# Moving the result's store, the semaphore clear and the last wait of a log-sum-exp kernel to SyncE

## Chip, cores, metric

One core of a Trainium2 chip. The metric is the device time of one execution in microseconds, the median of several. Each execution also has a span: the time from the start of the kernel's first instruction to the end of its last one. Time minus span is therefore what lies outside the kernel's own instructions. All runs quoted were with a granted clock of 1.0.

## The reference

```python
batch, seq, dim = 32, 512, 1024          # x: float32
x_max = np.max(x, axis=axis, keepdims=True)
return (x_max.squeeze(axis) + np.log(np.sum(np.exp(x - x_max), axis=axis))).astype(np.float32)
```

So 67.11 MB are read and 64 KB written. The kernel leaves out the maximum (the inputs are normal draws) and computes log(sum(exp(x))).

## The kernel before

Each of 128 partitions holds 128 rows of 1024 values. SyncE loads them in 17 chunks into a ring of 51 rows; ScalarE takes the exponential, VectorE (for some rows ScalarE's own accumulator) sums, and ScalarE takes the logarithm in three pieces. The last piece covers the last 4 rows and ends all arithmetic. Then comes the part in question:

```python
    take_logs(late_row, NB, late[:, : NB - late_row], dves, acts)   # last logarithm, on ScalarE
    nc.scalar.wait_ge(act_done, acts)
    nc.scalar.dma_start(out=out_v, in_=res).then_inc(stored, 16)    # 128 rows of 512 B
    nc.scalar.sem_clear(range(used[0], used[-1] + 1))               # 19 semaphores to zero
    # ... (cut) the first load is moved ahead of the opening barrier ...
    tc.close()                     # emits two exit barriers over all five engines
    tc.compile()
    nc.gpsimd.wait_ge(stored, 16)  # behind the barriers: is the store in memory?
    nc.gpsimd.sem_inc(stored, -16)
```

In the program this gives: store, clear, two exit barriers (each engine reports to GpSimd, GpSimd releases all), and one last instruction on GpSimd that waits for the store. Hiding the barriers behind the flight of the store is already part of the kernel before.

The softmax here doesn't subtract the row's maximum and nothing guards it: scores larger than these inputs give would overflow.

## Time and profile before

| what | value |
|---|---|
| median time | 163.15 us (3 runs, 163.01 to 163.37) |
| span of the profiled run (its time 163.28) | 161.41 us |
| end of the last logarithm | 159.76 us |
| last of 16 landings of the store | 161.37 us |
| end of GpSimd's wait, which is the end of the span | 161.41 us |

The rows of a source line in the profile give the engine, the operation, a count, durations in ns (minimum/median/maximum) and the first and last start in us. A "q" after an engine's name marks its instruction queue (waits, barriers, DMA issues), which is not counted as busy. The barriers consist of DRAIN and EVENT_SEMAPHORE instructions, with which the engines report, wait and are released. "Landing" is the time from the issue of a transfer to the last report that its data have arrived. The lines that carry the argument stand in the prediction. Behind the end of the span the trace holds one more thing, the times of semaphore updates; the prediction reads them too.

### The profile page before, as it was taken

The numbers are of one execution on the slowest core, as the hardware profiler recorded it, in microseconds if no ns is written. First come the engines' busy times: TensorE is split into PE (matmuls) and PEld (weight loads), VectorE is DVE, ScalarE is ACT, GpSimd is POOL, SyncE is SP. The second block draws the span as 40 slices with busy tenths as digits, with TensorE's granted clock in tenths as the row PEclk, the third lists the DMA queues.
The fourth block names the chain that finished last, engine by engine and source line by source line (L and its number), as shares of the span: only waits on it lengthen the run. The fifth ranks groups of instructions, "written<-read, shape, count | busy, mean of one in ns | idle before, by whom it ended". The sixth has DMA issues, their size and how long they took to land.

```text
span 161.4 us, 149 instructions
## 1 busy us (share of the span) xinstructions
DVE 121.0 (75%) x46; ACT 115.1 (71%) x40; POOL 0.2 (0%) x4
## 2 busy tenths in 40 slices
DVE  0028000003999999999999699999999999999892
ACT  3170005996079960999519993999199999999995
POOL 0000000000000000000000000000000000000000
DMA  6999699989989989989979999999999999999990
GB/s 256 508 487 457 289 472 520 406 374 520 422 357 520 406 374 520 406 374 520 406 341 455 455 455 439 422 422 422 430 429 429 418 426 415 427 430 417 403 394 24
DMA packets 2592, 67.18 MB, mean 416 GB/s; under 512 B 288, under 2 KB 416, under 8 KB 928
## 3 DMA queue, kind: packets, MB, share of 16 engines
q1 hardware_dynamic: 2448, 67.11, 96.9%
q10 hardware_dynamic: 144, 0.07, 0.1%
HBM read 67.11 MB, written 0.07 MB: 416 GB/s over the span
## 4 chain that ended last, share of the span: by engine, by line
DMA 49%; DVE 29%; ACT 20%; issue 0%
DMA ring<-in_x_dram 49%; DVE sums L154 29%; ACT ring L134 17%; ACT ring L161 3%; ACT res L105 0%
## 5 line engine op out<-in xcount | busy, mean ns | idle before, releaser
L154 DVE TENSOR_REDUCE sums<-ring 128x8 f32<-128x8192 f32 (+5 forms) x14 | 111.2, 7995 | 37.3 <-ACT ring L134 37.2
L134 ACT ACTIVATE ring<-ring 128x8192 f32<-128x8192 f32 (+6 forms) x18 | 104.4, 5835 | 43.9 <-DMA ring<-in_x_dram 43.8
L141 DVE CUSTOM_DVE_ANT_0 ring<-ring 128x512 f32<-128x512 f32 x16 | 9.9, 688 | 0.0
L161 ACT ACTIVATE ring<-ring 128x1024 f32<-128x1024 f32 x9 | 9.3, 1041 | 0.0
L119 ACT ACT_TABLE_LOAD x1 | 1.3, 1283 | 0.8 <-PEq L215 0.8
L161 ACT ACTIVATION_READ_ACCUMULATOR ring<-ring 128x1 f32 x9 | 1.5, 172 | 0.0
L141 DVE DVE_READ_ACCUMULATOR2_ANT sums<- 128x1 f32 x16 | 1.3, 84 | 0.0
L105 ACT ACTIVATE res<-sums 128x81 f32<-128x81 f32 (+1 forms) x2 | 0.5, 246 | 0.0
L105 ACT ACTIVATE res<-late 128x4 f32<-128x4 f32 x1 | 0.2, 173 | 0.0
L215 POOL MEMSET const-bfloat16-1.0<- 128x1 bf16 x1 | 0.1, 103 | 0.0
L215 POOL MEMSET const-uint8-127<- 128x1 uint8 x1 | 0.1, 102 | 0.0
L215 POOL MEMSET const-float32-0.0<- 128x1 f32 x1 | 0.1, 100 | 0.2 <-issue 0.2
L215 POOL MEMSET const-float32-1.0<- 128x1 f32 x1 | 0.1, 99 | 0.0
## 6 DMA issues: line engine op xcount, KB each, us to landing
ring<-in_x_dram SPq DMA_DIRECT2D x1, 7680.0 KB, 25.2
ring<-in_x_dram SPq DMA_DIRECT2D x1, 7168.0 KB, 28.6
ring<-in_x_dram SPq DMA_DIRECT2D x1, 6656.0 KB, 35.7
ring<-in_x_dram SPq DMA_DIRECT2D x1, 4608.0 KB, 20.2
ring<-in_x_dram SPq DMA_DIRECT2D x2, 2048.0 KB, 16.1
ring<-in_x_dram SPq DMA_DIRECT2D x1, 3584.0 KB, 28.3
ring<-in_x_dram SPq DMA_DIRECT2D x1, 2560.0 KB, 27.3
ring<-in_x_dram SPq DMA_DIRECT2D x4, 512.0 KB, 27.0
```

The lines of the kernel that those rows point to most:

```text
L105: nc.scalar.activation(out=res[:, lo:hi], in_=src, func=Ln).then_inc(act_done, 1)
L119: nc.scalar.preload_act_table_set("natural_log_exp_and_others")
L134: nc.scalar.activation(out=ring[:, s + lo : s + hi], in_=ring[:, s + lo : s + hi], func=Exp).then_inc(act_done, 1)
L141: nc.vector.tensor_tensor_reduce(out=ring[:, s + j, : D // 2], in0=ring[:, s + j, : D // 2], in1=ring[:, s + j, D // 2 :], scale=1.0, scal ...
L154: nc.vector.reduce_sum(out=sums[:, row + lo : row + hi], in_=ring[:, s + lo : s + hi], axis=AX).then_inc(dve_done, 1)
L161: nc.scalar.activation(out=ring[:, s + j], in_=ring[:, s + j], func=Exp, accum_out=total(row + j),).then_inc(act_done, 1)
L215: nc = _bacc.Bacc("TRN2", target_bir_lowering=False, num_devices=1)
```

## The change

Its intent: let the engine that has been idle since the last load issue the store, clear the semaphores, and also stand in the last wait, in place of ScalarE and GpSimd. Nothing else is touched.

```diff
-    nc.scalar.wait_ge(act_done, acts)
-    nc.scalar.dma_start(out=out_v, in_=res).then_inc(stored, 16)
-    nc.scalar.sem_clear(range(used[0], used[-1] + 1))
+    nc.sync.wait_ge(act_done, acts)
+    nc.sync.dma_start(out=out_v, in_=res).then_inc(stored, 16)
+    nc.sync.sem_clear(range(used[0], used[-1] + 1))
 ... (cut)
-    nc.gpsimd.wait_ge(stored, 16)
-    nc.gpsimd.sem_inc(stored, -16)
+    nc.sync.wait_ge(stored, 16)
+    nc.sync.sem_inc(stored, -16)
```

## The prediction

> **What bounds the kernel now.** I read the page first, then the chain that ended last in order of time, then line by line what happens after the last arithmetic, because the change touches nothing ahead of it.
>
> ```profile
> span 161.4 us, 149 instructions
> ...
> DVE 121.0 (75%) x46; ACT 115.1 (71%) x40; POOL 0.2 (0%) x4
> ...
> DMA packets 2592, 67.18 MB, mean 416 GB/s; under 512 B 288, under 2 KB 416, under 8 KB 928
> ...
> DMA 49%; DVE 29%; ACT 20%; issue 0%
> ```
>
> Loading 67.11 MB at 416 GB/s fills 161.3 us by division: the body is bound by the input transfer, with VectorE and ScalarE close behind. The load queue's packets take 96.9% of 16 engines' span. None of this is touched. The end of the chain in order of time:
>
> ```profile
> 158.46 1.11 ACT ring L161 x2
> 159.57 0.02 issue
> 159.59 0.17 ACT res L105
> ```
>
> The arithmetic ends at 159.76 us, yet the span is 161.4. The missing 1.64 us is the store and the wait for it. Four lines show it, each from the view of one source line:
>
> ```profile
> L173 ACTq DMA_DIRECT2D out_dram<-res x1: 373/373/373, 159.8 to 159.8; - x1
> ...
> DMA to landing us min/median/max: 1.6/1.6/1.6
> ```
> ```profile
> L176 ACTq EVENT_SEMAPHORE_RANGE_CLEAR  x1: 119/119/119, 160.2 to 160.2; - x1
> ```
> ```profile
> L196 POOLq EVENT_SEMAPHORE  x4: 17/17/17, 160.4 to 160.8; - x4
> L196 SPq DRAIN  x3: 7/7/123, 130.7 to 160.6; - x3
> ...
> L196 SPq EVENT_SEMAPHORE  x2: 17/17/17, 160.5 to 160.8; - x2
> L196 ACTq EVENT_SEMAPHORE  x2: 17/17/17, 160.5 to 160.8; - x2
> ```
> ```profile
> L198 POOLq EVENT_SEMAPHORE  x1: 17/17/17, 161.4 to 161.4; - x1
> ```
>
> The reader is to see an order: the store's issue on ScalarE at 159.8, the clear at 160.2, two exit barriers finished by about 160.9, and GpSimd standing alone until its wait for the store passes at 161.4. That wait, not the barriers, closes the span. SyncE has only waited since its last load:
>
> ```profile
> L97 SPq DMA_DIRECT2D ring<-in_x_dram x17: 327/365/779, 0.0 to 130.2; - x17
> ...
> SPq L196 <- PEq L196: 29.9, 2, 29.6
> ```
>
> **Beyond the span.** The trace also keeps the times of semaphore updates after the span. On one low semaphore, which no instruction of the kernel touches, two groups of nine stand there, in us from the span's start: 161.138, 161.172, 161.970, 162.014, 162.037, 162.136, 162.174, 162.210, 162.257; and 163.046, 163.080, 163.119, 163.163, 163.186, 163.284, 163.322, 163.356, 163.403. Between them all other semaphores are cleared in five blocks. The last update, 163.40, is close to the measured 163.28 us of the profiled run, so I take this closing part to be in the metric.
>
> **What the Trainium skill says.** "Runtime: NRT & Kernel Launch", section "The ~15µs preamble/postamble breakdown", lists after the kernel a sync barrier (about 1.5 us), a semaphore reset and another barrier, and calls the barrier a serpentine over five engines with 44 ns per hop and 8 hops. The trace agrees: nine updates are five engines out and four back, and the ready second group takes 0.36 us with hops of 23 to 98 ns. "Perfetto Trace Analysis", section "Per-instruction lifecycle", says that the window shown for a DMA from SyncE or ScalarE holds descriptor generation, not the data movement; here 0.37 us is shown and the landing takes 1.6. "DMA: Bandwidth & Descriptors", section "Issuing engines are not separate DMA queues", says that DMAs of all issuers run on the same 16 engines, and that another issuer saves only sequencer time. No run has tested that for this store; the isolated load issues on SyncE (minimum 327 ns, against 373) bear on the sequencer part.
>
> **The change part by part.** The built order shows the move of exactly two instructions from ScalarE's end to SyncE's, the store and the clear; VectorE and GpSimd are unchanged there. The closing wait goes from GpSimd to SyncE.
>
> 1. The start of the store. It waits for the last logarithm's semaphore. On ScalarE the issue began 30 ns after the end of that activation; the pieces called "issue" where one engine hands to another are also 0.02 us. SyncE has been idle since 130.7 us and has nothing ahead of it. Difference: 0.
> 2. The issue. One of 0.33 us (the minimum on SyncE, which the loads issued alone have) for one of 0.37: minus 0.04 us if the data starts with it. The same 128 rows of 512 B; all loads ended long before, so nothing contends. I count minus 0.02, half, because the two forms are not alike.
> 3. Landing and wait. Unchanged, 1.6 us from issue: SyncE's wait should pass at about 161.37, and the span should be about 161.4.
> 4. Clear and barriers. The 0.12 us clear and the branch now lie on SyncE ahead of its barrier; the barriers shift by at most 0.2 us. They ended 0.5 us before the landing (160.9 against 161.39), so this is hidden.
> 5. The closing. Here is the gain. In the first closing group the first two updates come before GpSimd's wait ends, and the third stands still until 161.970: 0.56 us after GpSimd's last instruction ended (161.41). In the second group the same hop takes 39 ns. So I read GpSimd as the third of the five and the one all waited for; SyncE, I infer, is the fifth. GpSimd freed from its wait is done with its barrier at about 160.9 to 161.0 and reaches its update at about 161.5, still ahead of the landing plus SyncE's own way. TensorE, which ended at 160.90, made its update at 161.14, 0.24 us after. If SyncE needs like TensorE 0.24 us from its last instruction (161.39), it arrives at 161.63. Its update then stands at about 161.65, against 162.037 before: minus 0.39 us. All that follows (return, reset, second group, 1.37 us) is a chain from there and moves with it.
>
> Sum: minus 0.02 and minus 0.39, about minus 0.4 us. The term from TensorE is an estimate for an engine that I have not seen there, so I shade it to minus 0.35: 163.15 - 0.35 = 162.8 us, 0.2%.
>
> **The rivals.** *SyncE is as slow on the way out as GpSimd.* With 0.56 us its update is at about 161.95, against 162.037: minus 0.09, and about 163.05 us. For it: I see only GpSimd's and TensorE's own way. Against it: SyncE's queue entries in the barriers are short (7 ns drain against 34 to 41 on GpSimd). *GpSimd's way remains the bound*, with 0.56 us after a barrier that ends late: about 161.5 is 0.1 earlier than SyncE's estimate, so it may cost a little if the barriers slip, no more. *The store from SyncE is slower*: busy issues on SyncE took up to 779 ns; that would add up to 0.4 and give about 163.2. Against it: that was among queued loads at the start, this one is alone. *The tail of SyncE becomes the wait*: if its branch stalled for over 0.5 us, the barriers would pass the landing. Its first drain after the last load was at 130.7, immediately after the last issue, so no stall shows. *The gain is outside the metric*: then the time stays at 163.15.
>
> **Range and chances.** The three runs of before span 163.01 to 163.37. The mechanisms leave 162.7 to 163.2, and 0.15 us of scatter on the low side gives 162.55 to 163.2. Two per cent is 3.3 us, twice the whole stretch from the last arithmetic to the end of the span; nothing moved is that large. Chances: faster 0.01, same 0.98, slower 0.01.
>
> **What would show it.** Right: a span of 161.3 to 161.5 with the store now in SyncE's queue, an issue of 0.33 to 0.37, a landing of 1.6 after the issue, both barriers over before the landing, SyncE's wait the last instruction; and among the later updates, hops three and four early (about 161.5) and hop five alone late, 0.2 to 0.3 us after the wait. Wrong: a landing of over 1.8 us, a barrier that ends behind it, hop five 0.5 us or more behind the wait, or an earlier closing with an unchanged measured time. A load phase that differs in the trace would be scatter, as no instruction of it changed.

## The result, and the profile after

The changed kernel takes **162.55 us** (median of 6 runs, 162.46 to 162.77) against 163.19 us (6 runs, 162.96 to 163.37). The ratio is 0.9963 with a 95% interval of 0.995 to 0.9976. Ratios here are not quite the ratio of the medians. At the threshold of 2% that is "same"; it is a small gain all the same, of 0.60 us by the ratio (0.0037 times 163.19).

The end of the chain, in order of time (start, duration, what), for the changed kernel:

```profile
158.28 1.11 ACT ring L161 x2
159.39 0.02 issue
159.41 0.17 ACT res L105
```

The last logarithm ends at 159.59 us instead of 159.76, in a part that did not change. Hold on to that 0.18 us: it is scatter, as the section on the experiments shows. The lines of the store, the clear, the barriers and the last wait, changed kernel:

```profile
L173 SPq DMA_DIRECT2D out_dram<-res x1: 348/348/348, 159.6 to 159.6; - x1
...
DMA to landing us min/median/max: 1.6/1.6/1.6
```
```profile
L176 SPq EVENT_SEMAPHORE_RANGE_CLEAR  x1: 64/64/64, 160.0 to 160.0; - x1
```
```profile
L196 POOLq EVENT_SEMAPHORE  x4: 17/17/17, 160.2 to 160.6; - x4
L196 SPq DRAIN  x3: 7/7/27, 160.1 to 160.4; - x3
```
```profile
L198 SPq EVENT_SEMAPHORE  x1: 17/17/17, 161.2 to 161.2; - x1
```

The store goes out through SyncE, with the issue 25 ns shorter; it lands 1.6 us later, as before. The barriers finish by 160.7, before the landing. The wait at the end is now SyncE's. How long it stood there is in the view of waits of SyncE's queue (who waited for whom, total us, times, longest):

```profile
SPq L173 <- ACT res L105: 29.1, 1, 29.1
SPq L198 <- SPq L198: 0.5, 1, 0.5
```

The first line replaces the 29.6 us that SyncE spent in the exit barrier before: it now waits for the last logarithm. The second is half a microsecond alone behind the barriers, waiting for its own store.

Up to here almost nothing is gained: from the end of the last logarithm to the end of the span it is 1.647 us before and 1.611 after. The rest is behind the span. These are the updates of the closing semaphore, on which the engines report one after the other; the step from one update to the next is called a hop below. They are given in us counted from the end of each kernel's span, so negative ones happened while the last wait still stood (from the trace's semaphore records, the first group of nine and the last update of the second group):

```
update       1       2       3       4       5       6       7       8       9     last
before   -0.271  -0.237   0.561   0.605   0.628   0.727   0.765   0.801   0.848   1.994
after    -0.222  -0.187   0.018   0.061   0.133   0.183   0.221   0.257   0.303   1.451
```

Before, the third update comes 0.56 us after GpSimd's last instruction, and everything queues behind it. After, GpSimd has been free since its last barrier instruction; its update comes at 0.018, again 0.562 us after that instruction, and the fifth update, SyncE's, comes 0.133 us after SyncE's wait.

The whole difference between the two profiled runs, to the last update of the trace, is 163.403 - 162.648 = 0.755 us. It splits into 0.176 from the body (scatter), 0.036 from the last logarithm to the end of the wait, 0.495 from the wait to the fifth update (0.628 against 0.133), and 0.048 from the fifth update to the last (1.366 against 1.318).

### The profile page after: what moved, and what is told of

Its sections match the earlier page's. It is cut to its first block, busy times and chain, and to the rows that moved or that the text cites. A ratio compares the mean times of both kernels' runs of the same rounds, so it can differ in the third digit from the quotient of the medians.

```text
span 161.2 us, 149 instructions
## 1 busy us (share of the span) xinstructions
DVE 121.0 (75%) x46; ACT 115.1 (71%) x40; POOL 0.2 (0%) x4
## 4 chain that ended last, share of the span: by engine, by line
DMA 49%; DVE 29%; ACT 20%; issue 0%
DMA ring<-in_x_dram 49%; DVE sums L154 29%; ACT ring L134 17%; ACT ring L161 3%; ACT res L105 0%
```

## The experiments

The theory after the result: the gain belongs to the **last wait**, not to the store. The engines report in a fixed order at the program's end; what counts is the place of the waiting engine in this order and its own way there. The rival: the gain is that of the store's issue and of a ScalarE relieved of it. All kernels gave correct results.

**1. The wait alone.** Store and clear as before, on ScalarE.

```diff
-    nc.gpsimd.wait_ge(stored, 16)
-    nc.gpsimd.sem_inc(stored, -16)
+    nc.sync.wait_ge(stored, 16)
+    nc.sync.sem_inc(stored, -16)
```

> Only the closing wait moves to SyncE; store and clear stay on ScalarE. Theory (the way from the closing wait to the end is shorter on SyncE, 0.13 us against 0.56 plus two hops on GpSimd): about 0.50 us below the kernel before, 162.65 to 162.75; the fifth closing update 0.13 us after SyncE's wait. Rival (the gain comes from the store's issue on SyncE): within 0.1 us of the kernel before.

Measured 162.35 us against 162.90, ratio 0.9963 (0.995 to 0.9977), the ratio of the full change. The fifth update comes 0.133 us after the wait. The time is below the expected range, because the kernel before, too, was faster on this chip than expected.

**2. The store alone.** Store and clear on SyncE, the wait on GpSimd.

```diff
-    nc.sync.wait_ge(stored, 16)
-    nc.sync.sem_inc(stored, -16)
+    nc.gpsimd.wait_ge(stored, 16)
+    nc.gpsimd.sem_inc(stored, -16)
```

(This diff and those of 3 and 4 are against the changed kernel.)

> Only store and clear move to SyncE; the wait stays on GpSimd. Theory: 0.03 to 0.1 us below the kernel before (issue 0.35 for 0.37, landing as before), third closing update 0.56 us after GpSimd's wait. Rival (the store's issue is what counts): 0.5 us below the kernel before.

Measured 162.77 us, ratio 0.9986 (0.9974 to 0.9999). The trace gives 1.604 us from the last logarithm to the end of the wait (1.647 before), and again 0.561 us to the third update and 1.994 to the last. So the store's move is worth about 0.04 us, and the time's 0.23 us (0.0014 times 163) is largely scatter of the span. The rival falls.

**How the scatter is taken out.** Every run lists its span. In 11 runs of the kernel before the spans go from 160.9 to 161.4 us and the times from 162.79 to 163.30, but time minus span stays within 1.84 to 1.92. No instruction differs among those runs, so the half microsecond is run-to-run variation of the body. The spans are listed to 0.1 us, so a single difference is good to 0.05 us only; in the profiled runs, whose spans are known to the nanosecond, it is 1.871 us for the kernel before and 1.333 for the changed one. From here on I compare time minus span, and in the trace the stretch behind the last logarithm.

**3. The wait on VectorE, TensorE and ScalarE.** The changed kernel, with `nc.sync` in the two last lines replaced by `nc.vector`, `nc.tensor` or `nc.scalar`.

```diff
-    nc.sync.wait_ge(stored, 16)
-    nc.sync.sem_inc(stored, -16)
+    nc.vector.wait_ge(stored, 16)       # e3; nc.tensor in e4, nc.scalar in e5
+    nc.vector.sem_inc(stored, -16)
```

> The changed kernel with the closing wait on VectorE, by the theory the fourth of the five in the closing chain. Its own way out was not seen. If it is 0.2 us, the fourth update comes 0.2 us after the wait and the fifth 0.02 later: 0.1 us above the changed kernel and 0.5 below the one before. The marks ahead of the fourth must be early (the third at about 161.2 us). Rival (any engine but GpSimd is the same): equal to the changed kernel.

> The changed kernel with the closing wait on TensorE, by the theory the first in the closing chain. Its way out was 0.24 us and four hops (34, 39, 44, 23 ns) follow: the fifth update 0.38 us after the wait, so 0.24 us above the changed kernel and about 0.35 below the one before; all nine updates after the wait. Rival (any engine but GpSimd is the same): equal to the changed kernel.

> The changed kernel with the closing wait on ScalarE, by the theory the second in the closing chain. Three hops (39, 44, 23 ns) follow its update; its own way out was not seen, I guess 0.15 to 0.2 us. So the fifth update 0.26 to 0.3 us after the wait, and the measured time minus the span 1.46 to 1.50 us (1.33 in the changed kernel, 1.88 before); only the first update is early. Rival (place in the chain does not matter, only each engine's own way out): fifth update under 0.2 us after the wait.

Each kernel's last instruction stands on the engine asked for; here TensorE's (the queue is called PEld), ScalarE's and VectorE's, from the view of the wait's source line in each of the three runs:

```profile
L198 PEldq EVENT_SEMAPHORE  x1: 51/51/51, 160.9 to 160.9; - x1
```
```profile
L198 ACTq EVENT_SEMAPHORE  x1: 17/17/17, 161.0 to 161.0; - x1
```
```profile
L198 DVEq EVENT_SEMAPHORE  x1: 21/21/21, 160.9 to 160.9; - x1
```

The closing, counted from the end of each span (from the semaphore records; time minus span over all runs of the kernel):

| last wait on | the waiting engine's update | us after the wait | fifth update | last | time minus span |
|---|---|---|---|---|---|
| TensorE | 1st | 0.279 | 0.419 | 1.783 | 1.63 to 1.68 |
| ScalarE | 2nd | 0.140 | 0.245 | 1.611 | 1.51 to 1.53 |
| GpSimd (store alone) | 3rd | 0.561 | 0.629 | 1.994 | 1.87 to 1.92 |
| VectorE | 4th | 0.183 | 0.206 | 1.570 | 1.43 to 1.49 |
| SyncE (wait alone) | 5th | 0.133 | 0.133 | 1.443 | 1.28 to 1.38 |

In the two rows of VectorE and SyncE the first positive number is not the waiting engine's: the third update of VectorE's run at 0.008 and the fourth of SyncE's at 0.008 belong to engines that were already on their way. Which update is the waiting engine's can be told from the runs together: GpSimd's comes 0.561 or 0.562 us after its last instruction wherever the wait stands (it is that third update of VectorE's run), VectorE's ready hop behind it takes 43 or 44 ns (the fourth of SyncE's run), and TensorE's and ScalarE's runs leave none and one update ahead of the wait. This settles the order: TensorE, ScalarE, GpSimd, VectorE, SyncE. The median times were 162.68, 162.46, 162.77, 162.53 and 162.35 us (ScalarE's from another call). "Any engine but GpSimd is the same" is wrong by 0.34 us between SyncE and TensorE in the last update. For ScalarE the rival of this run, that the place does not matter, falls as well: 0.140 us of its own way, 0.105 for three hops, 0.245 in all, just under what I had guessed (0.26 to 0.3). For TensorE I had expected the fifth update at 0.38; it came at 0.419, because TensorE's update came 0.279 us after its wait, where it comes 0.235 after its last barrier instruction in the kernel before. So TensorE's figure is not the same behind every instruction; why, no run shows.

**4. More work ahead of the barriers.** The clear done four times, in the kernel before and in the changed one.

```diff
-    nc.scalar.sem_clear(range(used[0], used[-1] + 1))
+    for _ in range(4):
+        nc.scalar.sem_clear(range(used[0], used[-1] + 1))     # e7: nc.sync, in the changed kernel
```

> The kernel before with the clear done four times on ScalarE: three more of 0.12 us and 0.03 us of gap, 0.44 us more ahead of the barriers. Theory: hidden behind the landing (slack 0.49 us), time minus span still 1.88, the time as before within 0.1 us. Rival (the barriers are on the path): 0.44 us longer.

> The changed kernel with the clear done four times on SyncE: three more of 0.06 us and 0.05 us of gap, 0.34 us more ahead of the barriers. Theory: the span stays, since the landing is later, but GpSimd's update (0.56 us after its last barrier instruction) moves from 161.2 to about 161.55 and takes over from SyncE's: time minus span 1.6 to 1.65, 0.3 us above the changed kernel. Rival (all that the barriers do is hidden now too): time minus span 1.33.

The changed kernel first. Time minus span became 1.56 to 1.63 us, and the ratio to the kernel before rose to 0.998 (0.9967 to 0.9994). The span's tail was unchanged (1.606 us behind the last logarithm), but GpSimd's last barrier instruction ended 1.313 us after it instead of 1.067; its update came at 0.269, as ever 0.562 us after that instruction, and the fifth at 0.337. That is the expected takeover, and it tells the margin: in the changed kernel VectorE's update at 0.061 leaves SyncE's, at 0.133, only about 0.05 us of slack once a hop of 0.023 is taken off. The delay was 0.246 us, not the expected 0.34. The trace has the parts: the three further clears, which start 0.09 to 0.10 us apart, add 0.28 us, and what frames them is 0.03 us shorter (the first drain takes 7 ns in place of 27, the issue 344 in place of 348).

```profile
L177 SPq EVENT_SEMAPHORE_RANGE_CLEAR  x4: 55/56/64, 159.6 to 159.9; - x4
```
```profile
L197 SPq DRAIN  x3: 7/7/7, 160.0 to 160.3; - x3
```

The kernel before with four clears took 163.07 us against 162.83, time minus span 2.05 to 2.15. **This I had not expected.** In its trace the theory holds: the wait ends 1.645 us after the last logarithm (1.647), the third update comes at 0.562, the last at 1.991. The measured time grew by about 0.22 us without any of that moving (the ratio, 1.0011 with 0.9996 to 1.0026, does not show it clear of the scatter; time minus span does). Runs 7 and 8 go after it.

**5. Two stores.** Meant to beat both kernels: 124 columns are stored after the second to last logarithm, 4 at the end, and the clear stands behind the barriers.

```diff
@@ behind the second to last logarithm
+            nc.sync.wait_ge(act_done, acts)
+            nc.sync.dma_start(out=out_v[:, :late_row], in_=res[:, :late_row]).then_inc(stored, 16)
@@ at the end
-    nc.sync.dma_start(out=out_v, in_=res).then_inc(stored, 16)
-    nc.sync.sem_clear(range(used[0], used[-1] + 1))
+    nc.sync.dma_start(out=out_v[:, late_row:], in_=res[:, late_row:]).then_inc(stored, 16)
@@ behind the barriers
+    nc.sync.sem_clear(range(used[0], used[-1] + 1))
-    nc.sync.wait_ge(stored, 16)
-    nc.sync.sem_inc(stored, -16)
+    nc.sync.wait_ge(stored, 32)
+    nc.sync.sem_inc(stored, -32)
```

> Meant to beat the changed kernel: 124 of 128 columns are stored after the second to last logarithm, 4 columns at the end, and the clear stands behind the exit barriers ahead of the wait. Theory: the last landing is bound by a fixed latency, so only the packets' part (0.35 us) can shrink: last logarithm to wait 1.5 us for 1.61, time minus span 1.33 or a little less, so 0.1 us below the changed kernel, in the trace and hardly in the time. Against it: pieces of 16 bytes may take longer, or the early store may still be in flight; then 0 or worse.

Half of it came true. The profile of this run shows both stores, and a shorter landing for the last one:

```profile
L133 SPq DMA_DIRECT2D out_dram<-res x1: 348/348/348, 158.3 to 158.3; - x1
L175 SPq DMA_DIRECT2D out_dram<-res x1: 343/343/343, 159.6 to 159.6; - x1
...
DMA to landing us min/median/max: 1.4/1.5/1.6
```

The wait ended 1.468 us after the last logarithm (1.611). The time was 162.42 us against 162.83, ratio 0.9972 (0.9959 to 0.9984), so no better than the changed kernel's 0.9963, and time minus span rose to 1.42 to 1.50: GpSimd's barrier part ended at 1.058 us, no earlier, and its update at 1.058 + 0.562 = 1.620 now came after SyncE's wait. To the last update it is 3.053 us from the last logarithm against 3.062: nothing won. Removing the clear from before the barrier did not help either, because SyncE's drain behind the issue grew to 123 ns where it was 27, and ended 0.180 us after the issue's end, as in the changed kernel (0.181):

```profile
L195 POOLq EVENT_SEMAPHORE  x4: 17/17/17, 160.2 to 160.6; - x4
L195 SPq DRAIN  x3: 7/7/123, 160.0 to 160.4; - x3
```

**6. The store inside the barrier.** So GpSimd must get through the barriers sooner. Here the last store (and its wait) is put in SyncE's stream between its two parts of the first exit barrier, its report and its wait for the release.

```diff
@@ added to run 5, behind tc.compile()
+    mine = [k for k in first.instructions if "SP" in str(k.engine)]
+    at = max(n for n, k in enumerate(mine) if k.opcode == "DMACopy")
+    moved = mine[at - 1 : at + 1]
+    first.instructions = [k for k in first.instructions if not any(k is m for m in moved)]
+    closing = nc.main_func.blocks[-1]
+    steps = closing.instructions
+    own = [n for n, k in enumerate(steps) if k.engine == moved[0].engine and k.opcode == "Drain"]
+    closing.instructions = steps[: own[1] + 1] + moved + steps[own[1] + 1 :]
```

Beside it the changed kernel was run again.

> The changed kernel again, beside the next three. Time minus span 1.33 us (1.88 before), fifth closing update 0.13 us after SyncE's wait; about 0.55 us below the kernel before if the spans scatter alike.

> The two stores of the run before, with SyncE's last store placed between its two parts of the first exit barrier, so that GpSimd need not wait for its issue and the 0.18 us of drain behind it. Theory: GpSimd's last barrier instruction ends 0.7 to 0.8 us after the last logarithm (1.06 there), its update is out of the way, SyncE's stands 0.13 us after its wait, 1.60 us after the last logarithm (1.74 in the changed kernel, 1.69 with two stores). 0.1 to 0.15 us below the changed kernel. Against it: the second drain on SyncE waits behind the issue all the same, then 0 to 0.05.

The changed kernel repeated: 162.68 us against 163.26, ratio 0.9958 (0.9944 to 0.9971), time minus span 1.28 to 1.39, fifth update at 0.135. In the new kernel GpSimd's part of the barriers begins beside the store's issue and not behind it:

```profile
L175 SPq DMA_DIRECT2D out_dram<-res x1: 343/343/343, 160.0 to 160.0; - x1
```
```profile
L195 POOLq EVENT_SEMAPHORE  x4: 17/17/17, 160.0 to 160.6; - x4
```

Its time is 162.52 us, ratio 0.9954 (0.994 to 0.9967), time minus span 1.29 to 1.37. GpSimd was done 0.670 us after the last logarithm, SyncE's wait ended at 1.467 and its update came 0.130 later, at 1.597. To the last update it is 2.907 us, against 3.054 in the changed kernel beside it: 0.147 us shorter in the trace. The times of the two do not separate (their intervals overlap almost wholly), since the body scatters by more than that. So it is better by its trace and not shown to be by its time.

**7 and 8. The 0.22 us that the trace does not show.** Two variants of the kernel before: one with six needless waits on long-landed loads at the first logarithm, which makes three more instructions on ScalarE at 128 us; one with the clear done twice.

```diff
+            for k in range(6):                     # e10
+                nc.scalar.wait_ge(landed[k], 16)
```
```diff
+    for _ in range(2):                             # e11
         nc.scalar.sem_clear(range(used[0], used[-1] + 1))
```

> The kernel before with three more instructions on ScalarE, all waits long satisfied, at the first logarithm (at 128 us), none at the end. In the four-clears variant of the kernel before, time minus span grew by 0.22 us though the closing in the trace did not. If the number of ScalarE's instructions did that, time minus span is 2.1 here too; if the clears did, 1.88.

> The kernel before with the clear done twice. Closing in the trace as before (2.0 us). If each clear costs a share of the 0.22 us that the four-clears variant lost, time minus span is about 1.95; if it is a step that comes with a barrier that ends near the landing, 1.88.

With three more instructions far from the end, time minus span is 2.11 to 2.15 us (163.60 us, ratio 1.0016, 0.9997 to 1.0036); the closing in the trace is as before (fifth update 0.629, last 1.995). With two clears it is 1.89 to 1.91 (163.39 us, ratio 1.0002, 0.9983 to 1.0021). So the 0.22 us come without any further clear and with the barriers where they were. In all 14 profiled runs, before and after included, the measured time is 0.11 to 0.13 us less than the time to the last update in the trace, except in these two, where it is 0.11 to 0.12 us more. These two have 54 instructions of ScalarE in the trace, all others 49 to 52. A step of 0.24 us goes with the length of ScalarE's program, between 52 and 54 instructions. It does not go with the length of all programs together: these two have 152 instructions in the trace, and so has the changed kernel with four clears, where the step is absent. Why, and where in time it lies, stays open; no record shows it. That the length is the cause is not shown either, since only two kernels have the step.

## Why the prediction was right or wrong

That the time stays within 2%, the sign and the place of the gain were right, but 162.55 us is at the very edge of the range. The prediction's mechanisms alone went down to 162.7; that the result lies inside is owed to the 0.15 us added for scatter. The gain was sized too small: 0.35 us stated, 0.60 measured.

1. *Start of the store, difference 0.* Right: 26 ns after the logarithm's end (31 before).
2. *The issue, minus 0.02.* Right in kind: 348 ns for 373 (343 to 348 in all runs with the store in one piece on SyncE, so not the 327 of a lone load). With the landing it made 0.036 us in the two profiled runs, and from the last logarithm to the end of the wait 1.60 to 1.62 us against 1.64 to 1.65 in the other runs with the whole store in one piece (1.66 with the wait on TensorE). The loads had not "ended long before": in the trace before the last one landed at 158.39 us, 1.4 us ahead of the store's issue. Nothing was in flight all the same. "DMA: Bandwidth & Descriptors", section "Issuing engines are not separate DMA queues", on which the prediction rests here, holds for this store: it moved the same packets (128 of 512 B) and landed 1.6 us after its issue from either engine.
3. *Landing 1.6 us.* Right; it still closes the span.
4. *Clear and barriers hidden.* Right, and the delay of up to 0.2 us did not occur: GpSimd's last barrier instruction ends 1.067 us after the last logarithm, 1.054 before. The clear takes 64 ns on SyncE against 119 on ScalarE and hides behind a drain that takes until 0.18 us after the issue anyway.
5. *The closing, minus 0.39.* The mechanism was right, third and fifth update as named, and shown by experiments 1 to 3. The mis-sized term is the way out of SyncE, which I took from TensorE as 0.24 us: **it is 0.133 us**. So the stretch from the wait to the fifth update shrank by 0.495 us. The prediction's figures make 0.37 for it (0.628 to 0.26); its 0.39 is taken from the span's start and holds the 0.02 us of the earlier wait, which its sum then counts a second time. I had all that follows as one chain of unchanged length; it was 0.048 us shorter, the hop after SyncE's own late update being 50 ns in place of 99. GpSimd's update I had at 161.5; it came at 161.215, for the barriers ended at 160.65, earlier than the 160.9 to 161.0 that I allowed (0.18 us of this is the body's scatter). Why GpSimd needs 0.56 us and SyncE 0.13, no run shows.
6. *Shading to minus 0.35.* This went the wrong way. The sum of what was measured outside the body is 0.036 + 0.495 + 0.048 = 0.58 us, near the 0.60 of the ratio.

Of the rivals, "SyncE is as slow as GpSimd" failed (0.133 against 0.56). "GpSimd's way remains the bound" failed in the changed kernel by 0.05 us, and came true with four clears and with two stores. "A slower store", "a tail that stalls" and "a gain outside the metric" failed: the trace shows none of the first two, and the time followed the closing updates in every kernel whose ScalarE program was no longer than 52 instructions.

## What to carry to other kernels

All of this was measured on one kernel. When a kernel has been tuned to where only the end is left, ask which engine stands in the last wait: the program is over only when the slowest engine has reported, so give that wait to the engine that reports last and leaves fastest (here SyncE, 0.13 us, where GpSimd takes 0.56), and get GpSimd through its last instruction early. Measure such tenths of a microsecond as time minus span or from a common event in the trace, since the body's run-to-run scatter of half a microsecond hides them. A shorter wait is worth nothing once another engine's report is next in line; look for its slack before shortening further.

## What the Trainium skill lacked or had wrong

- "Runtime: NRT & Kernel Launch", section "The ~15µs preamble/postamble breakdown", describes the barrier ahead of the kernel as a serpentine across five engines, with 44 ns per hop and eight hops. The prediction took it over to the barrier behind the kernel, and the trace agrees: the ready second group takes 0.357 us for eight hops. The page lacks the order of the engines and each one's own way to its update. The runs show TensorE 0.279, ScalarE 0.140, GpSimd 0.561, VectorE 0.183, SyncE 0.133 us from the end of the wait to the engine's update, in this order. Single hops of the ready group were 23 to 98 ns.
- The same section gives about 1.5 us for the semaphore reset behind the kernel; the five blocks of clears in the trace before took from 162.15 to 162.82 us counted from the span's start, 0.67 us.
- No page has what a clear of a range of semaphores costs: for 19 of them 119 ns on ScalarE, 64 on SyncE; nor that SyncE's drain behind a DMA issue lasts until 0.18 us after the end of the issue, so that a clear between the two is free.
- No page has the step of 0.24 us in measured time that came with 54 rather than 52 ScalarE instructions, with no trace of it in the records.
